# Second chunk's output projection by seven block products, with its weight factors made in steps behind keys and attention

## The chip, the cores and the metric

The kernel runs on one core of a Trainium2 chip. The metric is the device time of one execution in microseconds. The profile comes from one execution taken by the hardware profiler; times inside it are counted from the start of its span.

## The reference, cut to what matters

The layer works on x of 2048 positions by 1024 channels in float32. The part that is changed is the projection `@ w_out[l]` of the sum of two gated branches; what follows it is the norm whose result feeds the up projection.

```python
h = rmsnorm(x, attn_norm[l])
z = h @ w_in[l]                       # pool | q | k | v | gate_pool | gate_attn
gates = jax.nn.sigmoid((z[..., o4:] + b_gate[l]).astype(jnp.float32))
g_pool, g_attn = gates[..., :D_MODEL], gates[..., D_MODEL:]
a = pool_mixer(u_pool, w_pool[l], pool_scale[l])
b = swa_sink_attention(q, k, v, sinks[l])

x = x + (g_pool * a + g_attn * b) @ w_out[l]

h = rmsnorm(x, ffn_norm[l])
up = causal_depthwise_conv(h @ w_up[l], conv_w[l], conv_b[l])
gate, val = up[..., :D_FF], up[..., D_FF:]
x = x + (jax.nn.silu(gate) * val) @ w_down[l]
```

## The kernel before

Activations lie with channels on the 128 partitions and positions along the row. The 2048 positions are worked on in two chunks of 1024 (`c` = 0 and 1), each in two halves of 512 columns (`N0`, `N1`). The 1024 channels are eight tiles of 128. A product in float32 is made of three matmuls in a reduced format: each operand is split into a high part (ACT copy) and a low part (DVE subtraction), and high·high, high·low and low·high are summed (`mm3`, line 262, and `product`, line 1170).

Each chunk passes through these stages:

- `mixer`: keys and values block by block, then 32 attention items (four groups of eight blocks). Between an item's scores, probabilities and values TensorE works on *fillers*, projections of queries, pooled channels and gates. The gate projections of some channel tiles are left for `gates`.
- `gates`: for each channel tile in `UNITS[c]`, the two gate projections as seven block products (a Strassen-Winograd scheme: seven products of half-size blocks instead of eight, with sums of blocks as operands). Then `combine` makes the mixed branch of that channel tile and stores it in DRAM (`xd`).
- `out_proj`: the output projection, classic. For each half of the columns and each of the eight output tiles `m`, 24 matmuls (eight channel tiles by three) go to one PSUM bank. DVE adds the residual (line 1090), ACT scales by the norm's gain (line 1091) and squares, and the result is stored in `x2d`. Weights come through `stream`: raw slab into buffer `R`, split into `U`. The last channel tiles, 0 and 1, come straight from SBUF for the first half (`x0`, lines 1395 and 1396).
- In the second half of `out_proj`, `norms` closes the sum of squares of the first half on TensorE (`rstd`, line 629), POOL raises it to the power -1/2, `spread` (line 640) spreads it over the partitions into PSUM, and `right_first` scales and splits the operands of `up` (`normed`, line 1126; `parted`, lines 1043 and 1044).
- `up`: the up projection, convolution and gate for 22 feature tiles, by seven block products each. Its first units need the operands B11 and B21, then T1 to T4 and B22 (`right_t1` to `right_t4`), all made by DVE and ACT as the first units run. The first two units' weight factors are read from DRAM (`Kept`).
- `Down`: the down projection.

The order on each engine is laid out ahead of the run by a scheduler that goes by program order as priority and takes work that is ready; `tc.issue_after` puts instructions behind a given one on its engine. Each engine then works strictly in that order. All plain transfers are issued by SP in one queue; accumulating transfers by POOL. Buffers come from pools: `up` (tag U, 19 of 8 KB a partition), `rp` (R, 3 of 4 KB), `fp` (F, 4), `mp` (M, 5), `qp` (Q, 6). PSUM has two banks each for tags f, a and t, and one pair for s. A transfer into a buffer is issued only when the buffer is free.

## Time and profile before

| | |
|---|---|
| median of 3 runs | 2409.88 us (2409.58 to 2410.88) |
| profiled execution | 2411.6 us, span 2409.9 us |
| TensorE (PE) busy | 2375.1 us, 99%, 11120 matmuls |
| DVE busy | 1885.8 us, 78% |
| ACT busy | 1180.4 us, 49% |
| POOL busy | 177.0 us, 7% |
| DMA | 400.77 MB, mean 166 GB/s |
| second chunk's keys | about 1233 to 1324 us |
| its attention, three groups and part of the fourth | 1324 to 1557 us |
| its output projection on TensorE | 1681.86 to 1771.02 us |

A line of the profile names engine, line of the kernel, instruction and operands by the program's tags, with times in microseconds unless marked ns. Matmuls are pipelined, so their listed lengths overlap; the distance between starts is what one costs.

### The profile page before, as it was taken

What the parts mean: (1) busy time and instruction counts of PE and PEld (TensorE: products, weight loads), DVE (VectorE), ACT (ScalarE), POOL (GpSimd) and SP (SyncE); (2) the same over time, 40 slices, a digit from 0 to 9 for tenths busy, and PEclk for the clock granted to TensorE, in tenths of its full rate; (3) what the DMA queues carried; (4) which work ended last, traced back from release to release, by engine and by line L of the source; (5) the groups of instructions that cost most, each with busy time, mean ns of one, the idle gap of its engine ahead of it and who ended that gap; (6) DMA issues with size and microseconds to landing.
All of it is one profiled execution on the core that took longest, in us unless ns stands there. A gap on an engine that the chain in (4) does not pass through costs nothing.

```text
span 2409.9 us, 30324 instructions
## 1 busy us (share of the span) xinstructions
PE 2375.1 (99%) x11120; PEld 1970.3 (82%) x11120; DVE 1885.8 (78%) x2916; ACT 1180.4 (49%) x2169; POOL 177.0 (7%) x122
## 2 busy tenths in 40 slices
PE   9999999999999999999999999999999999999999
PEld 8888887877888888788888888878888888888887
DVE  8687887876977777799945867787588777779994
ACT  7455455454555555543522544554546445554431
POOL 1123111000000000000002142200000000000000
PEclk9999999999999999999999999999999999999999
DMA  9767778588222333545244576665742222228421
GB/s 342 245 202 236 228 218 274 192 288 295 103 79 79 93 117 114 178 173 183 88 155 141 171 220 195 200 201 198 230 167 93 95 80 79 79 71 288 140 70 53
DMA packets 162597, 400.77 MB, mean 166 GB/s; under 512 B 14224, under 2 KB 50576, under 8 KB 152720
## 3 DMA queue, kind: packets, MB, share of 16 engines
q1 hardware_dynamic: 157664, 390.26, 47.8%
q0 software_dynamic: 4352, 8.39, 2.2%
q8 instruction: 87, 1.43, 0.2%
q14 instruction: 62, 0.51, 0.1%
q10 hardware_dynamic: 432, 0.19, 0.0%
HBM read 264.17 MB, written 134.61 MB: 165 GB/s over the span
## 4 chain that ended last, share of the span: by engine, by line
PE 53%; DMA 2%; DVE 2%; ACT 1%; issue 0%; POOL 0%; DVEq 0%; ACTq 0%; POOLq 0%; SPq 0%
PE f L262 11%; PE f L1170 11%; PE t L1170 6%; PE f L1637 4%; PE a L1637 4%; PE s L1637 4%; PE t L1637 4%; PE a L1170 3%; PE a L934 1%; PE a L262 1%; PE s L873 1%; DMA tad<-U 1%; PE t L906 0%; DMA U<-xT 0%; DMA F<-dd 0%; DMA U<-xd 0%
## 5 line engine op out<-in xcount | busy, mean ns | idle before, releaser
L262 PE MATMUL f<-U,U 128*128 128x512 f32 (+1 forms) x2880 | 674.5, 390 | 9.4 <-ACT U L245 5.3
L262 PEld LDWEIGHTS f<-U,U 128*128 128x128 f32 x2880 | 529.1, 188 | 120.5 <-ACT U L245 6.6
L1170 PE MATMUL f<-U,U 128*128 128x512 f32 x1872 | 446.9, 390 | 4.1 <-ACT Q L1188 3.8
L1170 PEld LDWEIGHTS f<-U,U 128*128 128x128 f32 x1872 | 350.4, 188 | 80.1 <-ACT Q L1188 6.0
L1236 DVE SCALAR_TENSOR_TENSOR M<-F,vc,M 128x1024 f32<-128x1024 f32 x176 | 225.1, 1281 | 140.8 <-ACT M L1233 140.5
L1170 PE MATMUL t<-U,U 128*128 128x512 f32 x1332 | 316.7, 391 | 0.6 <-ACT Q L1188 0.6
L1170 PEld LDWEIGHTS t<-U,U 128*128 128x128 f32 x1332 | 250.9, 189 | 53.3 <-ACT Q L1188 1.2
L358 ACT CAST U<-R 128x1024 fp32r<-128x1024 f32 x147 | 153.8, 1053 | 86.5 <-DVE R L387 42.3
L1170 PE MATMUL a<-U,U 128*128 128x512 f32 x756 | 183.9, 390 | 0.0
L359 DVE TENSOR_TENSOR U<-R,U 128x1024 fp32r<-128x1024 f32 x147 | 179.2, 1220 | 3.0 <-ACT U L358 3.0
L1170 PEld LDWEIGHTS a<-U,U 128*128 128x128 f32 x756 | 141.3, 188 | 29.4 <-ACT Q L1188 0.2
L1170 PE MATMUL f<-U,M 128*128 128x512 f32 x624 | 151.3, 390 | 2.1 <-DVE F L1214 2.0
L892 ACT ACTIVATE Q<-s,st,rq 128x128 f32<-128x128 f32 x256 | 113.7, 455 | 63.6 <-DVE st L889 63.2
L1170 PEld LDWEIGHTS f<-U,M 128*128 128x128 f32 x624 | 116.8, 188 | 27.7 <-DVE F L1214 3.6
L914 POOL TENSOR_SCALAR_AFFINE_SELECT M<-M 128x1024 fp32r<-128x1024 f32 x64 | 94.7, 1479 | 381.2 <-DVE st L894 245.0
L1222 ACT COPY F<-f 128x512 f32<-128x512 f32 x52 | 30.5, 586 | 182.7 <-PE f L1170 182.7
L1595 ACT CAST U<-U 128x1024 fp32r<-128x1024 f32 x76 | 79.0, 1051 | 83.4 <-PE s L1637 21.5
L1233 ACT ACTIVATE M<-F,vc 128x1024 f32<-128x1024 f32 x88 | 109.4, 1243 | 2.0 <-DVE F L1218 0.5
L1596 DVE TENSOR_TENSOR U<-U,U 128x1024 fp32r<-128x1024 f32 x76 | 91.9, 1218 | 2.8 <-ACT U L1595 2.6
L1595 ACT CAST F<-U 128x1024 fp32r<-128x1024 f32 x44 | 46.2, 1050 | 93.0 <-PE a L1637 63.5
L941 ACT COPY U<-a 128x512 f32<-128x512 f32 x64 | 37.6, 587 | 109.4 <-PE a L934 109.1
L1188 ACT COPY Q<-f 128x512 f32<-128x512 f32 x104 | 60.8, 585 | 50.8 <-PE f L1170 50.8
(281 smaller groups left out, 3728.5 us busy)
## 6 DMA issues: line engine op xcount, KB each, us to landing
R<-w_up SPq DMA_DIRECT2D x80, 512.0 KB, 3.7
actd<-M SPq DMA_DIRECT2D x44, 512.0 KB, 2.6
U<-w_down SPq DMA_DIRECT2D x88, 256.0 KB, 4.7
U<-actd SPq DMA_DIRECT2D x88, 256.0 KB, 5.0
qd<-U SPq DMA_DIRECT2D x64, 256.0 KB, 3.7
Q<-qd SPq DMA_DIRECT2D x64, 256.0 KB, 4.9
R<-w_out SPq DMA_DIRECT2D x32, 512.0 KB, 5.1
U<-kept_S SPq DMA_DIRECT2D x12, 1024.0 KB, 6.3
```

The costliest lines, as they stand in the source:

```text
L262: nc.tensor.matmul(out, a, b, start=(i == 0), stop=(i == n - 1))
L358: A.copy(t[:, 0], raw)
L359: V.tensor_sub(t[:, 1], raw, t[:, 0].bitcast(F32))
L892: A.activation(pr[:, h, :], sc[:, h, 0:P], AF.Exp, bias=nm[:, h:h + 1], scale=it["rq"][:, h:h + 1], accum_out=rs[:, h:h + 1])
L914: G.affine_select(own.rearrange("p a h q -> p (a h) q"), pa.bitcast(F32).rearrange("p a h q -> p (a h) q"), pattern=[[0, 8], [1, P]], base ...
L1170: nc.tensor.matmul(bank, a[:, x, k, :], b[k // 2][:, y, k % 2, :], start=(first and i == 0), stop=(i == 11), skip_group_check=True)
L1188: Up.last = A.copy(t, bank).ins
L1233: A.activation(y, u[:, 2:], AF.Identity, bias=cw[:, 3, m:m + 1], scale=cw[:, 2, m:m + 1])
L1236: V.scalar_tensor_tensor(y, u[:, j:j + T], cw[:, j, m:m + 1], y, op0=ALU.mult, op1=ALU.add)
L1595: A.copy(hi, src)
L1596: V.tensor_sub(lo, src, hi.bitcast(F32))
L1637: nc.tensor.matmul(into[m], u[:, 0, c_], v[:, 1], start=(first and j == 0), stop=(k == n - 1 and j == 2), skip_group_check=True)
```

## The change

In the second chunk (`c` = 1) the output projection is no longer done by `out_proj` but by `out_blocks`. The output tiles 0 to 3 and 4 to 7 are the two row halves, the channel tiles 4 to 7 ("one") and 0 to 3 ("two") the halves of the sum, `N0` and `N1` the column halves. Seven products of blocks, each 48 matmuls to four PSUM banks, replace the 384 matmuls of the classic form. Their order is A11·B11, A12·B21, S2·T2, S3·T3, A22·T4, S1·T1, S4·B22.

The left factors are made by `out_factors`, a generator of 32 steps: one step after each of the eight key blocks and each of the 24 items of the first three attention groups. A step loads two slabs of `w_out`, or combines and splits one factor of 512 columns and stores it in DRAM (`out_parts`, 2 MB for each of the seven). `Out.weights` reads two 1 MB tiles back for each product.

The right operands come from `xd` through `mixed`, for channel tiles 0 and 1 too. Four PSUM banks `x` sum products 1, 3, 4 and 5, four banks `y` hold product 2, then 6 and 7. `kept` copies `x` to SBUF at half scale and adds the residual by an accumulating transfer issued by POOL; `final` adds a bank to that, squares it and stores it to `x2d`. The result stays in SBUF as operand of `up` without the norm's gain, so `normed` applies gain and scale by two instructions of 512 columns (`Halves`). The order of the mixing units in the second chunk becomes 5, 2, 4, 3, 0, 1. The entries of `w_out` for the second chunk leave the weight stream.

```diff
-UNITS = {0: (5, 2, 3, 0, 1), 1: (5, 2, 3, 4, 0, 1)}
+UNITS = {0: (5, 2, 3, 0, 1), 1: (5, 2, 4, 3, 0, 1)}
...
-        out += [("out", m) for n in range(2) for m in range(KT)]
+        out += [("out", m) for n in range(2) for m in range(KT) if c == 0]
...
+PRODUCTS = (("A11", "B11"), ("A12", "B21"), ("S2", "T2"), ("S3", "T3"), ("A22", "T4"),
+            ("S1", "T1"), ("S4", "B22"))
...
+    out_parts = {name: dp.tile([P, 4, 2, 4, P], F32, f"wo_{name}") for name, _ in PRODUCTS}
+    def out_factors():
+        one, two = slice(4, 8), slice(0, 4)
+        for i in range(4):
+            g, v = (rp.tile([P, 8, P], F32, "R") for _ in range(2))
+            load(g, w_out[i])
+            load(v, w_out[i + 4])
+            def part(name, src, i=i):
+                t = rp.tile([P, 2, 4, P], F32R, "R")
+                A.copy(t[:, 0], src)
+                V.tensor_sub(t[:, 1], src, t[:, 0].bitcast(F32))
+                load(out_parts[name][:, i], t.bitcast(F32))
+            yield
+            part("A11", g[:, one])
+            yield
...
+            V.tensor_sub(v[:, one], g[:, one], v[:, one])
+            V.tensor_sub(v[:, two], v[:, two], v[:, one])
+            part("S3", v[:, one])
+            yield
...
     def normed(x, n, pb):
...
+        if isinstance(x, Halves):
+            for k in range(2):
+                t, m = x.parts[n][:, k], 2 * x.j + k
+                V.scalar_tensor_tensor(t, t, vc[:, V_FN + m:V_FN + m + 1], pb[:, 0:512],
+                                       op0=ALU.mult, op1=ALU.mult)
+            return
...
+        def weights(self):
+            name = PRODUCTS[len(self.w)][0]
+            ts = [up_.tile([P, 2, 2, 4, P], F32R, "U") for _ in range(2)]
+            for i, t in enumerate(ts):
+                load(t.bitcast(F32), out_parts[name][:, 2 * i:2 * i + 2])
+            self.w.append(ts)
+        def mul(self, i, banks, first=False, by_pair=False):
+            w, r = self.w[i], self.b[PRODUCTS[i][1]]
+            for n in range(8):
+                j, m = divmod(n, 4) if by_pair else divmod(n, 2)[::-1]
+                at = 0
+                for k in range(2):
+                    for a, b in ((0, 0), (0, 1), (1, 0)):
+                        nc.tensor.matmul(banks[m], w[m // 2][:, m % 2, a, (2 * j + k + 2) % 4],
+                                         r[j][:, b, k], start=(first and j == 0 and at == 0),
+                                         stop=(j == 1 and at == 5), skip_group_check=True)
+                        at += 1
+                yield n
+        def kept(self, h, n, banks):
+            x = self.xs[h, n] = up_.tile([P, 4, 512], F32, "U")
+            for m in range(4):
+                A.activation(x[:, m], banks[m], AF.Copy, scale=0.5)
+            for i in range(2):
+                m = slice(2 * i, 2 * i + 2)
+                G.dma_start(x[:, m], self.rest(h, n)[:, m], accum_op=ALU.add)
+        def final(self, h, n, m, bank):
+            x = self.xs[h, n][:, m]
+            V.scalar_tensor_tensor(x, bank, 0.5, x, op0=ALU.mult, op1=ALU.add)
...
+            load(x2d[4 * h + m][:, n * 512:n * 512 + 512], x)
+    def out_blocks(ob):
+        heads = [Kept(f) for f in PRE]
...
+        s = ps2.tile([P, T], F32, "s")
+        x = [s[:, 0:512], s[:, 512:T]] + [ps.tile([P, 512], F32, t) for t in "at"]
+        ob.weights()
+        ob.mix()
+        run(0, x, True, True)
+        ob.first(2)
+        right_t1(ob.m, ob.b, None)
+        ob.mix()
+        ob.kept(0, 0, x)
+        ob.weights()
+        ob.first(3)
+        y = [ps.tile([P, 512], F32, t) for t in "ffta"]
+        run(1, y, True, True)
+        t2s = right_t2(ob.m, ob.b, None)
+        ob.weights()
+        for m in range(4):
+            ob.final(0, 0, m, y[m])
+        run(2, x)
+        right_t3(ob.m, ob.b)
+        ob.kept(0, 1, x)
+        ob.weights()
+        run(3, x)
+        right_t4(ob.m, ob.b, t2s)
+        ob.residual(1, 0)
+        ob.kept(1, 1, x)
+        ob.weights()
+        for n in ob.mul(4, x):
+            if n % 2 == 1:
+                ob.final(1, 0, n // 2, x[n // 2])
+        right_b22(ob.m, ob.b)
+        ob.weights()
...
+        for n in ob.mul(5, y, True):
+            if n == 2:
+                stats(0)
+            if n == 5:
+                pb = whole(0)
+            if n % 2 == 1:
+                ob.final(1, 1, n // 2, y[n // 2])
+        xg = ob.pairs()
+        for j in range(2):
+            right_first(xg, b, j, pb)
+        for n in ob.mul(6, y):
+            if n == 0:
+                for j in range(2, 4):
+                    right_first(xg, b, j, pb)
+            if n == 3:
+                for f in range(2):
+                    heads[f].fetch("A11", "A12")
+                stream.ahead().step(1)
+            if n % 2 == 1:
+                ob.final(0, 1, n // 2, y[n // 2])
+        return xg, b, [lambda: stats(1), lambda: whole(1)], heads
...
-            if f == n - 1:
+            if f == n - 1 and c > 0:
+                ob = Out(c)
+                for _ in range(2):
+                    ob.mix()
+                ob.weights()
+            elif f == n - 1:
                 mixes = {j: mixed(j) for j in (3, 2, 1)}
...
+        parts = out_factors() if c > 0 else iter(())
...
+            next(parts, None)
             if n > 1 or n == c == 1:
                 turn(n - 1)
...
+            if group < 3:
+                with tc.issue_after(last):
+                    next(parts, None)
...
-        up(c, *out_proj(c, *ms), dn)
+        up(c, *(out_blocks(*ms) if c > 0 else out_proj(c, *ms)), dn)
```

More of the change, by code (lines that the diff above doesn't have):

```diff
@@ L1135, in right_t1 @@
             normed(xg[j], 1, pb)
[L1136 removed]
+            q11, q12 = half(xg[j], 0), half(xg[j], 1)
             V.tensor_sub(q11, q12, q11)
@@ L1173, in product, with __init__, mix, first @@
                 i += 1
+    class Out:
+        def __init__(self, c):
+            self.c, self.m, self.w, self.b, self.xs = c, [], [], {}, {}
+            self.accs = [[], []]
+        def mix(self):
+            j = 3 - len(self.m)
+            self.m.append(Halves(j, [mixed_half for t in [mixed(j)]
+                                     for mixed_half in (t[:, :, N0], t[:, :, N1])]))
+        def weights(self):
[4 more added lines that the diff above has]
+            self.w.append(ts)
+        def first(self, j):
+            right_first(self.m, self.b, j, None)
+        def mul(self, i, banks, first=False, by_pair=False):
[10 more added lines that the diff above has]
+                yield n
+        def rest(self, h, n):
+            return xT[4 * h * P:(4 * h + 4) * P, self.c * T + n * 512:self.c * T + n * 512 + 512] \
+                .rearrange("(k p) t -> p k t", p=P)
+        def kept(self, h, n, banks):
[5 more added lines that the diff above has]
+                G.dma_start(x[:, m], self.rest(h, n)[:, m], accum_op=ALU.add)
+        def residual(self, h, n):
+            x = self.xs[h, n] = up_.tile([P, 4, 512], F32, "U")
+            load(x, self.rest(h, n))
+        def final(self, h, n, m, bank):
+            x = self.xs[h, n][:, m]
+            V.scalar_tensor_tensor(x, bank, 0.5, x, op0=ALU.mult, op1=ALU.add)
+            accs = self.accs[n]
+            if not accs:
+                accs.append(fp.tile([P, 512], F32, "F"))
+                A.square(accs[0], x)
+            else:
+                sq = mp.tile([P, 512], F32, "M")
+                A.square(sq, x)
+                if h == 1 - n and m == 3:
+                    accs.append(sq)
+                else:
+                    V.tensor_add(accs[0], accs[0], sq)
+            load(x2d[4 * h + m][:, n * 512:n * 512 + 512], x)
+        def pairs(self):
+            return [Halves(j, [self.xs[j // 2, n][:, j % 2 * 2:j % 2 * 2 + 2] for n in range(2)])
+                    for j in range(4)]
@@ new lines, in out_blocks, with run, stats, whole @@
+    def out_blocks(ob):
+        heads = [Kept(f) for f in PRE]
+        def run(*a, **kw):
+            for _ in ob.mul(*a, **kw):
+                pass
+        s = ps2.tile([P, T], F32, "s")
[29 more added lines that the diff above has]
+        ob.weights()
+        stream.fetch(stream.used + 1)
+        stream.part(stream.used + 1)
+        norms, b = [], {}
+        def stats(n):
+            rstd(ob.accs[n], r2[:, 4 * n:4 * n + 4])
+        def whole(n):
+            return spread(r2[:, 4 * n:4 * n + 4], None)
+        for n in ob.mul(5, y, True):
[19 more added lines that the diff above has]
+        return xg, b, [lambda: stats(1), lambda: whole(1)], heads
@@ L1490, in gates @@
             old.combine()
-            if f == n - 1:
+            if f == n - 1 and c > 0:
+                for j in range(2):
+                    ob.first(j)
+            elif f == n - 1:
                 ms = {j: [parted(mixes[j][:, :, N0])] for j in (3, 2, 1)}
```

34 lines of the change are left out of this document (26 added, 8 removed).

## The prediction

> **What bounds the kernel now.** I read the page first, then the tensor engine alone in order of time around the second chunk's output projection, then stages, then the last unit before it and the first units after it.
>
> ```profile
> span 2409.9 us, 30324 instructions
> PE 2375.1 (99%) x11120; PEld 1970.3 (82%) x11120; DVE 1885.8 (78%) x2916; ACT 1180.4 (49%) x2169; POOL 177.0 (7%) x122
> ```
> The tensor engine is busy for 2375.1 of 2409.9 us. Only 34.8 us are idle in the whole run, so a gain must come from fewer matmuls, and anything that makes it wait shows one for one.
>
> ```profile
> 1657.06 2.88 PE L1170 MATMUL t<-U,U 128*128 128x512 f32 x12
> 1659.78 2.88 PE L1170 MATMUL f<-U,U 128*128 128x512 f32 x12
> ...
> 1681.86 5.38 PE L262 MATMUL f<-U,U 128*128 128x512 f32 x23
> 1687.57 49.53 PE L262 MATMUL f<-U,U 128*128 128x512 f32 x217 [0.33 <-ACT U L1395]
> 1736.93 0.95 PE L629 MATMUL a<-one,F 128*128 128x1 f32 x8
> 1737.74 13.23 PE L262 MATMUL f<-U,U 128*128 128x512 f32 x57
> 1750.81 0.60 PE L640 MATMUL s<-identr,M 128*128 128x128 f32 x4
> 1751.16 20.02 PE L262 MATMUL f<-U,U 128*128 128x512 f32 x87
> 1771.02 2.88 PE L1170 MATMUL f<-U,U 128*128 128x512 f32 x12
> 1773.74 0.28 PE L629 MATMUL a<-one,F 128*128 128x1 f32 x2
> ```
> Columns: start, us, engine, line, instruction, count, idle before it with what ended it. A group of twelve starts 2.72 us after the one ahead of it, so one matmul of 512 columns takes 2.72/12 = 0.2267 us (the mean of 390 ns that the page shows is the pipelined length). The second chunk's projection is 23 + 217 + 57 + 87 = 384 matmuls of line 262 from 1681.86 to 1771.02, 89.2 us; 384 x 0.2267 is 87.0. The other 2.1 us are, by the starts, two blocks of small matmuls (0.81 and 0.35 us) and about 0.6 us at the front, where the first channel tile waits for the last mixing unit's parts.
>
> ```profile
> 1324.00:1557.00 233.00, 231.44 (x1203) 195.90 (x1204) 177.93 (x355) 110.29 (x354) 62.11 (x38) 1.00 0.64 193
> 1657.00:1682.00 25.00, 24.97 (x110) 20.35 (x110) 18.41 (x21) 11.34 (x16) 0.00 (x0) 1.00 0.73 258
> 1682.00:1771.00 89.00, 88.67 (x397) 73.08 (x396) 56.27 (x79) 44.56 (x73) 1.04 (x1) 1.00 0.67 220
> ```
> The columns after the window's length are busy times: PE, weight loads, DVE, ACT, POOL; then the clock, the DMA share and GB/s. The clock is full in all three. In the projection DVE has 56.3 of 89 us and ACT 44.6; DMA is the fullest helper (0.67, and 0.73 just before).
>
> **The removed matmuls.** The new stage runs 7 products of 8 groups of 6 matmuls: 336 instead of 384. That is 48 x 0.2267 = **-10.9 us**. [...]
>
> **The front.** The first product is A11·B11. It needs channel tiles 4 to 7 only, whose units end well before 1681.9 in the new order 5, 2, 4, 3, 0, 1. The 0.6 us wait goes: **-0.6**. Late next are channel tiles 0 and 1, which now reach TensorE through DRAM: the second half of product 2 needs `first(3)`, and that needs the load of `mixed(0)` behind the last `combine`.
>
> ```profile
> 1685.28 1.94 SPq L239 DMA_DIRECT2D xd<-M  x2
> 1686.11 0.75 DVE L1387 SCALAR_TENSOR_TENSOR M<-M,vc,M 128x512 f32<-128x512 f32 x1
> ...
> DMA to landing us min/median/max: 2.0/4.0/9.9
> U<-xd SPq DMA_DIRECT2D x8, 1024.0 KB, 7.1
> L1043 ACT CAST U<-U 128x1024 fp32r<-128x1024 f32 x50 | 52.2, 1052 | 40.1 <-DVE U L1126 9.8 <-DVE U L1137 8.2 <-PE t L1170 7.1
> L1044 DVE TENSOR_TENSOR U<-U,U 128x1024 fp32r<-128x1024 f32 x50 | 60.6, 1219 | 7.5 <-ACT U L1043 7.2
> ```
> The last half is combined at 1686.9. Its store takes from 2.0 us, so it lands at about 1689.1, and the 1 MB load behind it takes 5 (an estimate for a quiet queue, the median is 7.1): 1694.1 to 1696.2. The copy to the high part takes 1.05 and the subtraction 1.22, which gives 1696.4 to 1698.5. TensorE reaches that half after 72 matmuls, at 1681.9 + 16.3 = 1698.2. So it is met or missed by little. The load and the weight loads of the next products share one queue, so I take **+1.2** with bounds of 0 and 4 (a load of 10 us). One product later `right_t2` has 2 to 3 us to spare, and the remaining operands (T3, T4, B22) are made a product or more ahead.
>
> **PSUM and the accumulated residuals.** `kept` reads four banks by ACT copies, and `final` reads four by DVE. Each bank is rewritten 8.2 us (six groups of 1.36) or more after its last matmul, and a copy takes 0.62 (line 245's row below). I count nothing for it; without that cover each would cost its own 0.6 us four times a product. The accumulating transfers run on POOL's queue, where nothing else stands but the small powers of the norm.
>
> ```profile
> q1 hardware_dynamic: 7010, 19.28, 71.0%
> GB/s 197 234 291 269 276 223 200 422 354 245 219 144 232 230 246 149 45 110 274 280 318 341 203 324 354 223 70 185 18 159 101 0 155 219 194 356 335 437 401 411
> q0 software_dynamic: 4352, 8.39, 2.2%
> tad<-U POOLq DMA_DIRECT2D x16, 512.0 KB, 7.8
> ```
> The first two rows are of the 82 us from 1690 to 1772, the others of the whole run. The stage moved 19.28 MB at a share of 0.71, so 331 GB/s while busy, with slices up to 437. Accumulating transfers are dearer: 8.39 MB took 2.2% of 2410 us on all engines, 158 GB/s, and half a megabyte 7.8 us to land. The new stage moves 12.6 MB of factors for products 2 to 7 (two of 1 MB each), 4.2 of x2d stores, 2.1 of heads, 2.1 of mixes, 1.0 of residual and 1.6 of up weights, 23.6 MB in all: 71 us at 331 GB/s. Another 3.15 MB are accumulated: 20 us. That is 91 us against a stage of 78. What saves it is the lead. Of the 19 buffers of `up`, the mixing units give back 14 operand tiles and their weights between 1657 and 1682, so by my count of buffers factors 1 to 3 are asked for before 1682 and each later pair two products (21.8 us) ahead of use, where a 1 MB load took 7.1. The accumulated blocks are wanted one to four products later. I count no stall beyond the 1.2 above, and keep this as a rival.
>
> **Norm and the start of up.** `stats(0)` now sums two accumulators instead of one: 0.81 us more on TensorE, **+0.8**. The parts of B for `up` were made over four channel tiles of the old second half. Now all four `right_first` calls stand behind `whole(0)`, six groups into product 6.
>
> ```profile
> L1090 DVE SCALAR_TENSOR_TENSOR M<-f,F 128x512 f32<-128x512 f32 x32 | 22.0, 687 | 33.7 <-PE f L262 27.9 <-issue 5.6
> L375 DVE TENSOR_TENSOR M<-R,M 128x512 fp32r<-128x512 f32 x49 | 33.9, 691 | 0.2 <-ACT M L374 0.2
> ...
> 1776.90 0.43 DVE L638 COPY M<-r 128x512 f32<-128x512 f32 x1 [1.13 <-POOL r L622]
> 1778.25 0.60 PE L640 MATMUL s<-identr,M 128*128 128x128 f32 x4
> 1778.89 2.35 DVE L1126 TENSOR_TENSOR U<-U,s 128x1024 f32<-128x1024 f32 x2 [1.56 <-PE s L640]
> 1795.43 1.21 DVE L1044 TENSOR_TENSOR U<-M,U 128x1024 fp32r<-128x1024 f32 x1
> 1796.70 1.01 PEld L1170 LDWEIGHTS f<-U,U 128*128 128x128 f32 x5 [0.31 <-DVE U L1044]
> ```
> From the stage's start the product ends lie 10.9 us apart. `stats(0)` runs at 54.4 + 4.1 = 58.5, and the scale is spread by about 65. From there DVE owes: two `final` of product 6 (0.69 + 0.69 each, 2.8), four `right_first` (two scalings of 512 columns, 0.75 by the timeline's row at 1686.11, and 1.22: 2.7 each, 10.8), four `final` with three sums of product 7 (4.8), and one weight part (1.2): 19.6 us. The stage ends at 336 x 0.2267 + 1.6 + 0.35 = 78.1, so the last square is there at 65 + 18.4 = 83.4, some 5.3 us into `up`; before, the sums ran 2.7 us in (1773.74). `u1.one` fills that gap. But behind it DVE goes without a pause from the scaling at 1778.89 to T2's last part at 1796.64, and TensorE already waits for that part at 1796.70 (0.31). The chain starts 2.6 later, less the 0.9 that the transposes had waited for TensorE (1777.33 to 1778.25), plus four scalings that are two of 0.75 instead of one of 1.2 (0.27 each, 1.1): 2.8, and a wait already stands at its end. **+2.8**; 0 if DVE's order puts the `final` steps ahead of the last two `right_first`, 5 if the weight parts queue in front too.
>
> **The factors in steps.** 28 parts (ACT copy 0.62, DVE subtraction 0.69 by line 375's row), 16 combinations (0.69), 8 loads of 0.5 MB and 28 such stores (18.9 MB, 57 us of DMA at 331 GB/s). That adds 30 us to DVE and 17 to ACT over 32 steps, eight behind keys and 24 behind attention.
>
> ```profile
> L245 ACT CAST U<-R 128x512 fp32r<-128x512 f32 x122 | 69.6, 620 | 9.5 <-DMA R<-w_out 4.3 <-DMA R<-w_poolT 2.9 <-issue 1.4
> ...
> 1322.00:1330.50 8.50, 7.68 (x39) 6.13 (x38) 8.30 (x18) 5.19 (x20) 1.03 (x1) 1.00 0.11 32
> 1424.00:1432.50 8.50, 8.50 (x45) 7.19 (x44) 8.27 (x17) 3.95 (x14) 3.11 (x2) 1.00 0.84 229
> 1543.00:1551.50 8.50, 7.82 (x41) 6.41 (x40) 8.36 (x16) 5.13 (x13) 2.04 (x1) 1.00 0.18 70
> ```
> In attention DVE is at 177.9 of 233 us; 24 steps add 23, which makes 86%. The DMA share goes from 0.64 to about 0.83. SP's queue gets 36 more issues; a store waiting for its part holds the query loads behind it, but these are asked for two items (17 us) ahead. `R` has three buffers and two hold the slabs, so each part waits for the store ahead of it to land, 4.0 us by the median of the `xd` row, out of some 8.5 us for one item. In the fullest stretches of that length DVE has 8.3 of 8.5 us already, and there a step pushes the chain from scores to values back by up to 1.3 us. Most of that is covered by projections on TensorE. **+1.0**, bounds 0 and 6 (a quarter of a microsecond lost at each of the 24 steps).
>
> **Sum.** -10.9 - 0.6 + 1.2 + 0.8 + 2.8 + 1.0 = -5.7 us. The profiled span is 2409.9 (its execution 2411.6 with what lies around it); the median of the runs is 2409.88, the same as the span. So 2409.9 - 5.7 = **2404.2 us**. All costs at their low ends give -10.7 (2399.2), all at the high ends -10.7 + 4 + 5 + 6 = +4.3 (2414.2).
>
> **Rivals.** *Full gain, 2399.2*: DVE's order and the load of channel tiles 0 and 1 both fit. For it: DVE and ACT are idle for 33 and 44 of the 89 us that the projection takes now, so they have room. Against it: the wait at 1796.70 already stands at the end of the DVE chain.
>
> *Attention crowded, 2409.2*: the full items spill onto TensorE what exceeds 8.5 us, 1.1 each in the three shown and the like in others, 6 us in all instead of 1.0. For it: two of the three stretches shown have TensorE at 7.7 and 7.8 of 8.5. Against it: over 1324 to 1557 TensorE lost 1.6 us in all, and the one at 1424 with 8.27 us of DVE lost none.
>
> *Transfers bound the stage, slower, 2417*: the place is products 2 to 5, the price 91 us of transfers against 78 of matmuls, +13 on the forecast; it decides once buffers come back so late that the factors lose their two-product lead. For it: the share before the stage is already 0.73. Against it: 2 MB of weights and one mix leave that stretch, factor tiles are 8 KB to a row, and slices of such loads show over 400 GB/s. [...]
>
> *The change doesn't do what it says*: if the projection's matmuls do not drop by 48, only the costs of 5.8 us less the front's 0.6 remain, 2415.1. The loops count 7 x 48, so hardly any chance.
>
> **Chances.** Forecast 0.46, full gain 0.21, attention crowded 0.19, transfers bound 0.12, no drop 0.02. A measurement of this kernel can tell about 0.2% from no change, 4.8 us, so faster means below 2405.1 and slower above 2414.7. The forecast's own range is 2401.5 to 2407; about three quarters of it are below 2405.1. Faster: 0.21 + 0.35 = 0.56. Slower: 0.12 + 0.02 = 0.14. The rest, 0.30, is no change. The range for 8 in 10 runs from 2398.8 to 2411.5: it takes in the full gain and the crowded attention and leaves out most of the transfer-bound case.
>
> **What would show it.** Matmuls of line 262 fall by 384, and 336 appear under the new `mul`. Right: they span about 79 us, the gap before product 2's second half is under 1.5 us, and the wait for DVE at T2 in `up` grows from 0.3 to about 3. Wrong: idle TensorE inside products 3 to 7 that ends on a DMA of `wo_` (transfers), more than 3 us of new waits on POOL or DVE between 1233 and 1557 (attention), or no longer wait at T2 (full gain).

## The result and the profile after

The changed kernel takes 2424.2 us (median of 4 runs, 2422.9 to 2425.6), the kernel before beside it 2410.4 (2409.6 to 2411.1). The ratio is 1.0056, with a 95% interval of 1.0044 to 1.0069: slower, by 13.8 us, and outside the range that was forecast (2398.8 to 2411.5).

The page after (its head and one group), and two stretches of the trace, attention and the block stage, which is the new output projection (columns as before: length, busy times of PE, weight loads, DVE, ACT, POOL; clock, DMA share, GB/s):

```profile
span 2421.1 us, 30322 instructions
PE 2370.1 (98%) x11080; PEld 1962.8 (81%) x11080; DVE 1907.9 (79%) x2948; ACT 1181.4 (49%) x2166; POOL 186.5 (8%) x128
...
L266 PE MATMUL f<-U,U 128*128 128x512 f32 (+1 forms) x2496 | 586.6, 390 | 9.6 <-ACT U L249 4.8
```
```profile
1314.00:1567.00 253.00, 242.67 (x1257) 202.85 (x1256) 205.31 (x403) 123.04 (x380) 64.40 (x39) 1.00 0.76 238
...
1689.00:1776.00 87.00, 82.38 (x360) 67.36 (x359) 48.23 (x59) 32.18 (x46) 8.40 (x7) 0.96 0.77 247
```
The matmuls went as counted: line 262's 2880 of the old page are 2496 of line 266, and TensorE is busy 5.0 us less. But the span is 11.2 us longer. TensorE is idle some 10 us in attention, and 4.6 us in the block stage, where the mean clock is 0.96 (1.00 in the projection before).

Where it was lost can be read from the starts of the stages on TensorE (first transpose of attention, first unit product behind it, first matmul of the output projection, first product of `up`), here for the first profiles (the kernels are told below). "Clock" is 1 minus the granted clock, summed over stretches of 1 us from 1300 us on to 10 us before the end; half clock while TensorE waits counts too, so it is the most that the clock can have cost.

| kernel | attention | gates | output proj. | rest | clock | span | median against before |
|---|---|---|---|---|---|---|---|
| before | 242.2 | 123.8 | 89.2 | 638.9 | 0 | 2409.9 | 2410.4 |
| after | 253.1 | 122.2 | 86.6 | 645.2 | 5.1 | 2421.1 | +13.8 |
| a_plain | 252.5 | 122.3 | 79.5 | 643.7 | 3.4 | 2412.7 | +5.2 |
| b_steps | 253.4 | 122.4 | 89.0 | 638.9 | 0 | 2420.1 | +9.4 |
| c_blocks | 242.8 | 123.0 | 85.6 | 646.5 | 5.1 | 2413.1 | +4.6 |
| d_both | 242.7 | 122.2 | 79.5 | 642.4 | 0 | 2402.4 | -3.6 |
| e_moves | 242.9 | 122.8 | 88.9 | 639.0 | 0 | 2409.6 | +0.2 |
| f_math | 249.6 | 122.8 | 89.0 | 639.2 | 1.7 | 2417.2 | +5.7 |

So the changed kernel loses 10.8 us in attention, wins 2.6 in the projection where 10 were expected, and loses 6.3 behind it. It wins 1.6 in the gates. The other 1.8 lie ahead of the change: in the first chunk the clock column, counted the same way, is 5.1 in the profile of before and 3.4 in that of after, and waits differ by some tenths.

Inside the block stage, rows picked from the timelines of PE, DVE, ACT and POOL, in order of time:

```profile
1689.30 2.88 PE L1260 MATMUL s<-U,U 128*128 128x512 f32 x12
...
1699.16 1.23 POOL L1277 DMA_DIRECT2D U<-xT  x1 [101.63 <-PE a L1260]
1712.12 0.69 DVE L1285 SCALAR_TENSOR_TENSOR U<-f,U 128x512 f32<-128x512 f32 x1 [4.93 <-DMA U<-xT]
1712.35 1.22 POOL L1277 DMA_DIRECT2D U<-xT  x1 [11.95 <-issue]
1719.22 2.88 PE L1260 MATMUL t<-U,U 128*128 128x512 f32 x12
1721.10 0.69 DVE L1285 SCALAR_TENSOR_TENSOR U<-t,U 128x512 f32<-128x512 f32 x1 [6.56 <-DMA U<-xT]
1721.71 1.22 DVE L1084 TENSOR_TENSOR U<-U,U 128x1024 fp32r<-128x1024 f32 x1
1721.83 0.63 ACT L1292 ACTIVATE M<-U 128x512 f32<-128x512 f32 x1 [6.62 <-DVE U L1285]
1724.70 1.07 ACT L1274 ACTIVATE U<-s 128x512 f32<-128x512 f32 x2
1725.82 8.63 PE L1260 MATMUL s<-U,U 128*128 128x512 f32 x24 [3.71 <-ACT U L1274]
1726.18 1.22 POOL L1277 DMA_DIRECT2D U<-xT  x1 [12.62 <-ACT U L1274]
1734.28 2.88 PE L1260 MATMUL a<-U,U 128*128 128x512 f32 x12
1737.26 1.22 POOL L1277 DMA_DIRECT2D U<-xT  x1 [9.86 <-issue]
1749.12 1.21 POOL L1277 DMA_DIRECT2D U<-xT  x1 [10.64 <-PE a L1260]
1757.11 1.22 POOL L1277 DMA_DIRECT2D U<-xT  x1 [6.78 <-issue]
```
Read it from the PE row at 1725.82 back. Product 4 waits 3.71 us for ACT's copies of product 3's banks (`kept`). ACT does them at 1724.70, because it works in order and ahead of them stand squares of `final`'s sums (line 1292). Those wait for DVE's `final`, and DVE waits in order for the accumulated residual, 4.93 and 6.56 us; T3's split (1721.71) stands behind it too. POOL's two transfers of one pair are 13 us apart with nothing between them. Over the whole stage the waits of DVE are:

```profile
DVE U L1285 <- DMA U<-xT: 20.2, 4, 6.6
```
(20.2 us in four waits.) The second thing in the PE row is its length: 24 matmuls take 8.46 us to the next start, where 24 x 0.2267 are 5.44. The granted clock there:

```profile
1720.00:1724.00 4.00, 2.10 (x10) 1.41 (x8) 2.90 (x4) 1.56 (x2) 0.00 (x0) 1.00 0.19 70
1724.00:1728.00 4.00, 2.18 (x5) 1.80 (x6) 3.24 (x5) 3.84 (x6) 1.22 (x1) 0.64 0.81 207
1728.00:1732.00 4.00, 4.00 (x11) 3.03 (x11) 1.58 (x2) 0.64 (x2) 0.00 (x0) 0.50 0.96 347
```
From 1725.1 to 1732 the clock is half. The first 0.7 us of that still lie in the wait; after it the matmuls lose 8.46 - 5.44 = 3.0 us. The wait of 3.71 us therefore cost 6.7.

Behind the stage:

```profile
1775.87 2.99 PE L1225 MATMUL f<-U,U 128*128 128x512 f32 x12 [0.91 <-issue]
1780.65 0.35 PE L669 MATMUL a<-one,F 128*128 128x1 f32 x2 [1.79 <-DVE F L1296]
...
1807.79 1.43 PE L1225 MATMUL f<-U,U 128*128 128x512 f32 x5 [1.82 <-DVE U L1084]
```
The sum of squares is late by 1.79 us, and behind it the clock is half for 3.4 us (1783 to 1787, 1.7 in the clock column); T2 is late by 1.82, where before it was 0.31.

In attention, what PE waited for, and then two of ACT's waits:

```profile
PE t L946 <- DVE Q L938: 4.4, 6, 1.9
PE s L913 <- ACT Q L932: 4.3, 4, 1.7
```
```profile
ACT R L406 <- DMA wo_A<-R: 7.0, 4, 3.1
...
ACT R L406 <- DMA wo_S<-R: 3.0, 3, 1.7
```
Before, the like rows of PE were 1.1 and 0.4 us in all. A factor step's copy waits on ACT until the store of the part before it has let the R buffer go, and ACT's exponentials stand behind it.

### The profile page after: what moved, and what is told of

Same layout as the page of the kernel before. It is cut to its first block, busy times and chain, and to the rows that moved or that the text cites. A ratio compares the mean times of both kernels' runs of the same rounds, so it can differ in the third digit from the quotient of the medians.

```text
span 2421.1 us, 30322 instructions
## 1 busy us (share of the span) xinstructions
PE 2370.1 (98%) x11080; PEld 1962.8 (81%) x11080; DVE 1907.9 (79%) x2948; ACT 1181.4 (49%) x2166; POOL 186.5 (8%) x128
## 4 chain that ended last, share of the span: by engine, by line
PE 47%; DVE 4%; DMA 3%; issue 3%; ACT 1%; POOL 0%; SPq 0%; POOLq 0%; DVEq 0%; ACTq 0%
PE f L1225 11%; PE t L1225 6%; PE f L266 5%; PE f L1846 4%; PE a L1846 4%; PE s L1846 4%; PE t L1846 4%; PE a L1225 3%; PE a L266 1%; DMA U<-xT 1%; DVE F L1030 1%; PE a L974 1%; PE s L1260 1%; DMA tad<-U 1%; PE s L913 1%
## 5 line engine op out<-in xcount | busy, mean ns | idle before, releaser
L266 PE MATMUL f<-U,U 128*128 128x512 f32 (+1 forms) x2496 | 586.6, 390 | 9.6 <-ACT U L249 4.8
L266 PEld LDWEIGHTS f<-U,U 128*128 128x128 f32 x2496 | 457.2, 188 | 105.2 <-DVE U L250 7.3
L1225 PEld LDWEIGHTS f<-U,U 128*128 128x128 f32 x1872 | 351.1, 188 | 83.5 <-ACT Q L1387 5.5
```

The lines of the kernel that those rows point to most:

```text
L266: nc.tensor.matmul(out, a, b, start=(i == 0), stop=(i == n - 1))
L1225: nc.tensor.matmul(bank, a[:, x, k, :], b[k // 2][:, y, k % 2, :], start=(first and i == 0), stop=(i == 11), skip_group_check=True)
```

## The experiments

**Two losses, taken away alone and together.** First the way of the residual:

```diff
         def kept(self, h, n, banks):
...
             x = self.xs[h, n] = up_.tile([P, 4, 512], F32, "U")
+            load(x, self.rest(h, n))
             for m in range(4):
-                A.activation(x[:, m], banks[m], AF.Copy, scale=0.5)
-            for i in range(2):
-                ... G.dma_start(..., accum_op=ALU.add)
+                V.scalar_tensor_tensor(x[:, m], banks[m], 0.5, x[:, m], op0=ALU.mult, op1=ALU.add)
```


> The changed kernel with one thing undone in the output stage: the residual of the three kept blocks comes by a plain load on SP's queue, and DVE adds half the product's bank to it, instead of four copies by ACT and two accumulating transfers by POOL. The factor steps in keys and attention stay. Theory A (the accumulating transfers run one after the other, each 9 to 13 us, and what waits for them on DVE, 20.2 us in four waits, holds ACT and the banks of products 4 to 7 and the start of the next stage): the waits of DVE on the accumulated blocks go, the output stage falls from 86.6 us to 79 to 81, the start of the next stage gives back 2 to 5 us more, total 2410 to 2416. Rival B (the stage is held by the bytes of 21 MB of factors and by DVE's own work, so the way the residual comes does not matter, and DVE even gets 12 instructions more): the stage stays at 85 to 89 us, total 2421 to 2427.

Measured: +5.2 us against before (ratio 1.0021, 1.0012 to 1.0030), so 8.6 better than the change. The stage takes 79.5 us, no product waits longer than this:

```profile
1707.81 2.56 PE L1260 MATMUL f<-U,U 128*128 128x512 f32 x10 [0.61 <-DVE U L1084]
```
Theory A holds, and with more bytes on the same queue and 12 instructions more on DVE. DVE still waits 9.7 us in three waits for the plain loads (20.2 in four before), but no product waits for what stands behind them. The gain behind the stage is smaller than it said (1.5 us, not 2 to 5).

Then the factor steps alone, with the old projection and the old order of units behind them:

```diff
-UNITS = {0: (5, 2, 3, 0, 1), 1: (5, 2, 4, 3, 0, 1)}
+UNITS = {0: (5, 2, 3, 0, 1), 1: (5, 2, 3, 4, 0, 1)}
...
-        up(c, *(out_blocks(*ms) if c > 0 else out_proj(c, *ms)), dn)
+        up(c, *out_proj(c, *ms), dn)
```


> The factor steps are made in keys and attention and stored as in the changed kernel, but the second chunk's output projection is the old one, with the old order of gates; the stored factors are not used. Theory (the steps cost what the trace of attention shows, +10.8 us, whatever the stage behind does with them): before plus 9 to 13 us, 2419 to 2424, of which attention shows 9 to 11. Rival (the growth of attention comes mostly of the new order of gates and of the later loads that the block stage brings with it): before plus 0 to 4 us, 2410 to 2415.

Measured: +9.4 us (1.0033, 1.0021 to 1.0046), attention 253.4 us, everything behind it as before:

```profile
1316.00:1558.00 242.00, 232.95 (x1208) 194.89 (x1206) 196.63 (x386) 118.61 (x369) 62.44 (x37) 1.00 0.75 239
```
and of before:

```profile
1316.00:1558.00 242.00, 240.44 (x1257) 203.47 (x1256) 186.54 (x369) 111.86 (x360) 62.28 (x39) 1.00 0.62 188
```
PE is busy for 233.0 us of the same 242, where it was 240.4, and DVE for 10 us more. The steps cost what attention shows; the order of gates and the later loads do not.

The block stage without the steps, and with both edits. Both runs load stored factors of the gates in place of those of `w_out`, so their output is not the reference's, and only their time counts:

```diff
-                load(t.bitcast(F32), out_parts[name][:, 2 * i:2 * i + 2])
+                load(..., kept[i]["A11", "A12"]...)
...
-        parts = out_factors() if c > 0 else iter(())
+        parts = iter(())
```


> The block products of the changed kernel without the making of their factors: no steps in keys and attention, and each product loads, in the same transfers, factors of the gates that are in DRAM already, so the output differs from the reference's. What is left is the change's own stage at its full price. Theory (10.8 us of the loss come of the steps): the changed kernel minus 9 to 12, 2411 to 2415, about the time of before, for the stage gains 2.6 us and the start of the next loses 6.2. Rival (the stage and its transfers cost more than the steps): 2417 to 2422.

> Both edits at once: no factor steps (factors of the gates are loaded in their place, so the output differs from the reference's), and the residual by plain loads with the sum on DVE. Theory (two losses that add: steps 10.8 us, accumulating transfers 8 to 13 us): 2398 to 2404, which is the full gain of 10.2 us that I had computed for 48 matmuls fewer and the x0 wait. Rival (the two share a cause, for example a DVE that is full in both places, so that taking both away gives no more than the larger one): 2408 to 2414.

Measured: +4.6 us (1.0017, 1.0008 to 1.0027) and -3.6 us (0.9979, 0.9970 to 0.9988). Taking away the steps wins 9.2, the accumulating transfers 8.6, both 17.4: the losses are separate and add. With both gone the stage takes 79.5 us, and the profiled run is 7.5 us under the profile of before; the median says only 3.6, 2.9 over the range that was expected: its ten runs lie between 2401.6 and 2408.8, with granted clocks from 0.999 down to 0.996. Behind the stage of the run with both edits one wait is new:

```profile
1788.95 1.43 PE L1225 MATMUL f<-U,U 128*128 128x512 f32 x5 [1.83 <-DVE U L1084]
```
It is the wait for T2 again.

**Work or transfers in the steps.** One run in which a step only moves data, and one in which it stores nothing:

```diff
-                t = rp.tile([P, 2, 4, P], F32R, "R")
-                A.copy(t[:, 0], src)
-                V.tensor_sub(t[:, 1], src, t[:, 0].bitcast(F32))
-                load(out_parts[name][:, i], t.bitcast(F32))
+                for h in range(2):
+                    load(out_parts[name][:, i, h], src)
```


> As the run with the old projection and the factor steps (attention 253.4 us against 242.2 before, total 9.4 us over before), but a step only moves data: it reads its slabs of w_out and stores the half slab twice to the factor's place, with no copy by ACT and no subtraction by DVE, so no factors are made (they are not used in this run either). Theory M (the steps cost by their transfers: 4 x 1 MB in, 28 x 0.5 MB out, buffers R held longer, later loads of queries, gates and inputs): attention 250 to 254 us, total 7 to 10 us over before. Rival W (they cost by the 28 copies on ACT and the 40 subtractions on DVE, put in order ahead of the chain of scores, probabilities and values): attention 242 to 245 us, total 0 to 3 over before.

```diff
-                load(out_parts[name][:, i], t.bitcast(F32))
```


> The other half of the same pair: the steps read their slabs and do all their work on ACT and DVE, but store nothing (so no factors are kept; they are not used here). Theory M: attention 242 to 246 us, total 0 to 4 us over before. Rival W: attention 250 to 254 us, total 7 to 10 over before. If both runs lie in the middle (246 to 249), the two add, and neither alone is the cause.

Measured: +0.2 us (0.9999, 0.9990 to 1.0009) and +5.7 (1.0027, 1.0016 to 1.0038), attention 242.9 and 249.6 us. The first does not test what it was meant to. With no engine's work to wait for, the scheduler put the transfers ahead, at 1120 to 1233 us, behind the down projection:

```profile
1120.00:1160.00 40.00, 40.00 (x176) 32.81 (x175) 39.50 (x59) 14.37 (x18) 0.00 (x0) 1.00 0.96 328
```
(before: a share of 0.33). It shows that 18.9 MB cost nothing there, not what they cost in attention. The second run does tell, and lies between its two theories: ACT's and DVE's work alone makes 7.4 us of attention. The stores, in the run with both, add 3.8 more (253.4 against 249.6), which fits the waits for R. The split is rough: 1.7 of the 7.4 are clock behind a wait of 1.95 us, and the attention of the run with both has no such piece. The medians give 5.7 for the work and 3.7 for the stores.

**Why the accumulating transfers run one by one.** Twice the scratch memory that the program asks for (`dynamic_dma_scratch_size`, 2048 for 1024), with one Q buffer of six given up for it:

```diff
-    qp = pool("qp", 6)
+    qp = pool("qp", 5)
...
-    nc = bacc.Bacc(..., dynamic_dma_scratch_size=1024)
+    nc = bacc.Bacc(..., dynamic_dma_scratch_size=2048)
```


> [...] In the changed kernel POOL issued its six accumulating transfers 13.2, 13.8, 11.1, 11.9 and 8.0 us after one another. If the small memory makes one wait for the one before it, the two of a pair come less than 3 us apart, DVE's waits on accumulated blocks shrink from 20.2 us to under 10 and the output stage from 86.6 to 80 to 83 us; in attention the lost Q buffer may cost some us. If each transfer waits for the one before for another reason, the spacing stays at 8 to 13 us and the stage at 86 to 88.

Measured: 2418.6 us (one run), and on POOL:

```profile
1700.25 1.23 POOL L1277 DMA_DIRECT2D U<-xT  x1 [102.06 <-PE a L1260]
1702.48 1.20 POOL L1277 DMA_DIRECT2D U<-xT  x1 [1.00 <-DVE U L1218]
1723.41 1.21 POOL L1277 DMA_DIRECT2D U<-xT  x1 [19.73 <-PE t L1260]
1726.28 1.22 POOL L1277 DMA_DIRECT2D U<-xT  x1 [1.66 <-ACT U L1274]
```
The first two pairs go out 2.2 and 2.9 us apart instead of 13.2 and 11.1, DVE waits 12.0 us for them, not 20.2 (under 10 was expected), and the stage falls to 81.4 us. It was that memory which made one transfer wait for the one before. The lost Q buffer does not show in attention (253.0).

**Other places for the factors.** The residuals are plain in all that follow. First, 16 steps behind the last group of the first chunk's down projection, with their subtractions on POOL, and 16 in keys; then with the copies on POOL too:

```diff
+                if self.c == 0 and g == len(self.groups) - 1:
...
+                    side[0] = G
+                    if at % 2 == 0 and at // 2 < 16:
+                        next(factor_steps, None)
...
-                V.tensor_sub(t[:, 1], src, t[:, 0].bitcast(F32))
+                side[0].tensor_sub(t[:, 1], src, t[:, 0].bitcast(F32))
```


> A version that should beat both: the residual by plain loads with the sum on DVE, and the factor steps moved out of attention. 16 of the 32 steps lie behind every second product of the last group of the first chunk's down projection (1120 to 1230 us, where POOL is idle and the transfers of the run that only moves data cost nothing), with their subtractions on POOL and the copies on ACT; the other 16 lie in keys, two behind each block of rows, on ACT and DVE. The output is the reference's. Theory (steps cost only where DVE, ACT and the chain of attention have no slack): attention falls from 252.5 to 242 to 244 us, the down projection and keys keep their times within 2 us, total 2403 to 2409, 2 to 7 us under before. Rival (POOL's subtractions slow DVE, which is 98% busy in the down projection, or ACT's copies wait for R buffers in order ahead of the next parts): the down projection grows by 4 to 10 us and eats the gain, total 2408 to 2416.

> As that run, but in the down projection POOL also makes the copies, so that ACT has no part in the 16 early steps and cannot wait for a buffer in order. Theory: 2403 to 2409, equal to it within 1 us, if ACT's waits there cost nothing. Rival: 2 us or more under it if ACT's waits held the down projection; 2 us or more over it if POOL, with twice the work, becomes late and the steps run into keys.

Measured: +14.0 us (1.0059, 1.0045 to 1.0073) and +18.0 (1.0077, 1.0064 to 1.0089). The rival, in both halves. Attention does fall to 243.2 us in both, but the first transpose of keys comes 17.4 and 21.9 us later than before. The same subtraction of the down projection, on DVE from 1120 to 1200 us, before and, in the first of the two, with POOL working beside it, and POOL's own (1120 to 1240 us):

```profile
L1596 DVE TENSOR_TENSOR U<-U,U 128x1024 fp32r<-128x1024 f32 x18 | 21.7, 1216 | 0.1
```
```profile
L1807 DVE TENSOR_TENSOR U<-U,U 128x1024 fp32r<-128x1024 f32 x15 | 22.5, 1517 | 0.9 <-ACT U L1806 0.9
...
L409 POOL TENSOR_TENSOR R<-R,R 128x512 fp32r<-128x512 f32 x14 | 24.7, 1768 | 190.5 <-ACT R L408 190.5
```
DVE's instruction takes 1517 ns for 1216, and DVE was 97% busy there before. It is not the transfers: in the run that only moves data the DMA share is 0.94 over these 80 us, and the instruction takes 1220 ns:

```profile
L1789 DVE TENSOR_TENSOR U<-U,U 128x1024 fp32r<-128x1024 f32 x18 | 21.7, 1220 | 1.2 <-ACT U L1788 1.2
```
ACT waited up to 16.2 us for a store to free R. PE lost 9.2 us in one wait on DVE at the start of keys.

Next, the plain blocks A11, A12, A22 stored by the first chunk's projection, which splits those slabs anyway, and S1 to S4 made in keys, two in a block; then with the parts in M buffers:

```diff
+                if c == 0 and n == 1:
+                    for name, k in (("A11", 4), ("A12", 0)) if m < 4 else (("A22", 0),):
+                        load(out_parts[name][:, m % 4], w[:, :, k:k + 4].bitcast(F32))
```


> A second try at a version that beats both, with no work on POOL and none in attention. The residual comes by plain loads. The 12 factors that are plain blocks of w_out (A11, A12, A22) are not made by steps at all: the first chunk's output projection splits the same slabs anyway, and in its second half stores the parts (6.3 MB) as it has made them. The other 16 (S1 to S4, 16 copies on ACT, 32 subtractions or additions on DVE, 8.4 MB out) are made in keys, two in each block of rows, half a block apart. Theory (keys has room: PE is 100% busy there with DVE at 59% and ACT at 32%, and the 8 steps that the changed kernel has there cost it nothing): keys stays at 82.5 us within 2, attention at 242 to 244, total 2404 to 2409, 2 to 6 us under before. Rival (16 steps wait for slabs and for the one R buffer left for parts, in order ahead of the keys' own chain, as the early steps of the two runs before did): keys grows by 4 to 12 us, total 2411 to 2420.

> As that run, with one thing else: the parts that a step makes lie in an M buffer (five of them) instead of the third R buffer, so that a step need not wait for the store of the one before it. Theory: equal to it within 1 us, if no step waits there. Rival: 2 us or more under it, if the waits for the store cost it; over it, if the M buffers are missed by the queries that are made in keys.

Measured: +5.3 us (1.0029, 1.0016 to 1.0041) and +8.9 (1.0038, 1.0025 to 1.0051). In the profile of the first, keys (82.5 us) and attention (242.5) are as before: 16 parts cost nothing in keys. This profile is of the fastest of its six runs (2411.8 us), with a span equal to that of before; what makes the median longer is not in it. The gain of the block stage is lost in the first chunk, whose stores filled the queue, and in the start of `up`; keys began 4.7 us later than before:

```profile
598.85 1.65 PE L1221 MATMUL f<-U,U 128*128 128x512 f32 x3 [2.49 <-DMA U<-kept_A]
```
In the second, keys takes 84.4 and attention 248.8 us, with 4.2 us of waits of PE on loads of made weights between the two.

Then the plain blocks split in the block stage, out of raw slabs; in a second run two of the three splits stand earlier:

```diff
+                if name[0] == "A":
+                    r = rp.tile([P, 2, 4, P], F32, "R")
+                    ... load(r[:, j], w_out[at + 2 * i + j][:, k:k + 4])
...
+                A.copy(t[:, :, 0], r)
+                V.tensor_sub(t[:, :, 1], r, t[:, :, 0].bitcast(F32))
```


> A third try at a version that beats both. The run before this one had keys at 82.5, attention at 242.5 and the block stage at 79.6 us in its profile, and lost 4.6 us in the first chunk's output projection, to the stores of A11, A12 and A22 (transfers 79% busy there against 57%, and a 2.5 us wait of PE on a late load behind them). Here these three factors are never stored: the block stage loads the slabs of w_out themselves (half the bytes) into R buffers, which it does not use otherwise, and splits them there, six copies of 1024 elements on ACT and six subtractions on DVE of 1.2 us. S1 to S4 are made in keys, two in a block. Theory: first chunk as before, keys and attention as before within 1 us, the block stage 79.5 to 82 us for DVE is 73% busy in it, the start of the next stage 3 to 5 us over before; total 2403 to 2408, 2 to 7 us under before. Rival (the 7 us more on DVE meet its full stretch at the end of gates and at the start of the block stage, and PE waits over 3 us on a split part): 2410 to 2416.

> The run that splits A11, A12 and A22 in the block stage, with the splits of two of them earlier: A12's slabs are loaded and split behind the last gate products (before the stage, where DVE was 62 to 85% busy), A22's are loaded one product earlier and split ahead of the T4 operands instead of behind them. Theory (PE's waits of 4.4 and 2.5 us and the two and one slow-clock windows behind them came of the place of these two splits): no wait of PE over 1 us in the stage, stage 79.5 to 82 us, total 2404 to 2410. Rival (DVE has no room for 7 us more there, wherever they stand): the waits move to product 1 or 3 or to the end of gates, total 2412 to 2419.

Measured: +8.1 us (1.0035, 1.0023 to 1.0047) and +4.1 (1.0015, 1.0006 to 1.0024). Keys and attention are as before in both. In the first, PE waits for `first(3)` in product 2, and again ahead of product 5, for `kept`'s sums of product 4, with 5.1 us of clock at the two. What ended last ahead of the second wait was no split but a load of the residual, for which DVE waited 3.43 us:

```profile
1704.69 4.63 PE L1269 MATMUL f<-U,U 128*128 128x512 f32 x10 [4.38 <-DVE U L1077]
...
1735.16 1.29 DVE L1284 SCALAR_TENSOR_TENSOR U<-s,U 128x512 f32<-128x512 f32 x2 [3.43 <-DMA U<-xT]
1736.59 4.58 PE L1269 MATMUL s<-U,U 128*128 128x512 f32 x12 [2.50 <-DVE U L1284]
```
The second run loses the later wait and keeps the first one, of 4.39 us: its raw slabs go into SP's queue ahead of the mixed channel tiles and wait there for R, and DVE waited 2.9 us for the load of these tiles (1688.70), from which on it worked without a pause up to the operand that PE missed. The stage took 92.4 us in the first and 86.4 in the second.

Last, all 28 parts in keys, 24 (A22 split in the block stage), and 20 (A11 and A12 stored by the first chunk):

```diff
             block_b(n)
+            next(parts, None)
...
                 turn(n - 1)
+            next(parts, None)
+            if n % 2 == 1:
+                next(parts, None)
```


> The run with plain residuals, with one thing else: all 28 factor steps in keys, three or four in each of its 8 blocks, none in attention. Theory (only the place counts: PE leads in keys, with DVE at 59% and ACT at 32% before, and 28 steps add 28 us of DVE and 18 us of ACT to 82 us): keys 82.5 to 84, attention 242 to 244, total 2404 to 2409. Rival (keys has its own bound: 14.7 MB out and 4.2 MB in beside its 12 MB is 380 GB/s, the steps wait for the one R buffer of parts, some 4 us each by the stores' time to landing, and push the last steps and the queries into attention): keys plus attention grow by 4 to 10 us, total 2411 to 2417.

> As that run with 24 steps in keys, three in a block: the four for A22 are left out, and the block stage loads the plain slabs for its fifth product and splits them there on ACT and DVE (1720 to 1730 us, where DVE is about half busy). Theory: keys 82.5 to 83.5, attention 242 to 243.5, the stage 79.5 to 81, total 2403 to 2408. Rival as in the run before, with 24 parts for 28: 2409 to 2415; or the split of A22 holds product 5 as the splits of the run with plain slabs held products 2 and 4 (4.4 and 2.5 us): 2409 to 2413 with keys and attention as in the theory.

> The run that stores the plain parts in the first chunk's output projection and makes S1 to S4 in keys, with one difference: the four parts of A22 are made in keys too (20 there, two or three a block), so that the first chunk stores 4.2 MB for 6.3. Theory: the wait on the late load in the first chunk falls from 2.5 us to under 1, keys and attention stay as they were with 16, total 2405 to 2411. Rival (20 parts in keys are over its bound): the loads of made weights and queries behind them come late, PE waits 2 us or more at the start of attention, total 2413 to 2420.

Measured: +14.1 us (1.0056, 1.0044 to 1.0069), +12.4 (1.0050, 1.0036 to 1.0063) and +14.1 (1.0054, 1.0042 to 1.0067). Keys itself stays at 82.5 us in all three. But the loads for the start of attention, which share SP's queue with the stores, come late. SP issues in order, and a store waits for DVE to finish its part. First the wait of PE with 24 parts, then the waits of SP's queue for parts, in us in all, times and the longest, from the start of keys to 1335 us, with 24 and with 16 parts:

```profile
1328.72 2.47 PE L266 MATMUL f<-U,U 128*128 128x512 f32 x5 [8.27 <-DMA U<-made_q]
```
```profile
SPq L243 <- DVE R L407: 42.0, 14, 6.7
```
```profile
SPq L243 <- DVE R L407: 19.3, 4, 8.0
```
Attention takes 261.2, 258.7 and 256.6 us, with 5.1, 6.8 and 3.4 us of clock in it. The rival holds: keys has its own bound. 16 parts fit with R buffers (with M buffers attention grew), 20 do not. No kernel that really makes its factors beat the kernel before.

## Why the prediction was wrong, by its own steps

**The removed matmuls, the front, `first(3)`: right.** The terms -10.9, -0.6, +1.2 and +0.8 give -9.5 for the projection. With plain residuals and no steps it went from 89.2 to 79.5 us, -9.7. The gap before product 2's second half was nil after the change, and 0.6 with plain residuals (priced at 1.2, forecast under 1.5). That the sum agrees to 0.2 us is in part luck, for this term was half of what was priced and some tenths elsewhere make up for it. (Of the 2.1 us beyond the matmuls that the prediction reads in the old projection, the three items it names make 1.8.)

**The start of `up`: the size right without the accumulating transfers, the place in part.** +2.8 forecast; +3.5 measured with both losses gone (638.9 to 642.4). The wait at T2 that was named grew from 0.31 to 1.83 us, not to about 3; another 0.87 us is a wait ahead of the spreading of the scale (line 680), and about 1 us is not located.

**PSUM and the accumulated residuals: the first step that failed.** The text said "I count nothing" and that the blocks "are wanted one to four products later". It had the right row (7.8 us for half a megabyte, 20 us in all) and then asked only whether POOL's queue was free. It did not ask who stands behind `final` on DVE. The transfers went out 8.0 to 13.8 us apart, so the last of six was issued at 1757. DVE stood still for 20.2 us, and behind it stood T3's split, the squares on ACT and, behind those, the copies that let the next product have its banks. That is 7.1 us in the stage and 1.5 at the start of `up` by the pair of runs, 8.6 in all where 0 was written.

**The clock: not in the prediction at all.** Of the 7.1 us 3.7 are the wait, 3.0 are TensorE at half clock behind it, and 0.9 are a gap ahead of `up`; the run with plain residuals has 0.6 of its own at product 2. Every wait was priced at its own length.

**The factors in steps: the second step that failed, by size and by bound.** +1.0 with bounds of 0 and 6 was written; attention grew by 10.8 and the runs with and without steps differ by 9.2 to 9.4. The mechanism was named: full stretches of DVE and the single R buffer for parts. It was priced as if the projections on TensorE covered it. The bound of a quarter of a microsecond a step came from no row; the row-based figure in the same paragraph, up to 1.3 us where a stretch is full, would have allowed far more. Measured in the profiles of attention, 7.4 us come with the work alone (1.7 of it clock), which PE shows as waits for DVE and ACT inside the chain of scores, probabilities and values, and 3.8 are added by stores. The rival *attention crowded* had the right place with 6 us.

**Transfers bound the stage: not shown.** It had the right sign for another reason. No product waited on a load of factors in the changed kernel or with plain residuals, though the latter's queue carried more. What had to do with transfers were six small ones on POOL.

**The sum.** From profile to profile: -9.7 + 7.1 in the projection, +6.3 behind it (3.5 of its own, the rest about the late sum of squares with its clock), +10.8 in attention, -1.6 in the gates, which the prediction did not touch, and -1.8 ahead of it all: +11.2. Most of the -1.6 is one wait of TensorE for DVE, before and after:

```profile
1602.36 3.01 PE L1170 MATMUL f<-U,M 128*128 128x512 f32 x12 [1.68 <-DVE F L1214]
```
```profile
1610.16 3.04 PE L1225 MATMUL f<-U,M 128*128 128x512 f32 x12 [0.50 <-DVE F L1413]
```
The second chunk's order of units cannot explain it alone, for with the old order the gates show -1.4 too and this wait is 0.4; why it shrinks stays open.

## What to carry to other kernels

Ask of each wait that a change adds what stands behind it in order on the waiting engine, and who waits for that; a transfer that is wanted "a product later" holds everything queued behind its reader. Where TensorE is 99% busy, price its waits above their length: in the six profiles named in the next section every wait of 2.78 us or more from 50 us on went with half clock for at least 3.4 us, and some shorter ones did, down to 0.86 us. Work moved out of a stage needs a place with room on all of its engines, its buffers and its queue at once, and only a run shows how much fits there (here 16 parts in keys, not 20).

## What the runs showed of the hardware that was not expected

**The clock falls in steps of 1.7 us.** In six profiles (before, after, the run that splits two of the plain blocks earlier, and those with 28, 24 and 20 parts in keys), away from the last 10 us, the clock goes to half for 3.4 us or a multiple of it: 1 minus the clock, summed over 1 us stretches, comes in pieces of 1.71, of 3.41 and, with the wait of 8.27 us in the run with 24 parts, of 6.83. Each stands in or behind waits of TensorE; in the changed kernel 3.41 with the wait of 3.71 us and 1.71 with the one of 1.79. Length alone does not decide. From 50 us on every wait of 2.78 us or more has a piece. Shorter ones have it or not: the same wait of 0.90 us near 561 us has one in the run with 24 parts and none in the profile of before, where a wait of 2.05 us (421 us) has none either. In the changed kernel the clock falls at 1725.1, 3.0 us into the wait of 3.71 us, but in the run with 24 parts a wait of only 0.86 us (it ends at 1782.29) has a piece. Because the first chunk has such waits too, two profiles of the same code there can differ by 1.7 us: a wait near 400 us has 3.41 before (2.79 us long) and 1.71 after (2.80).

**Accumulating transfers wait for one another** with `dynamic_dma_scratch_size` at 1024: pairs 13.2 and 11.1 us apart, 2.2 and 2.9 with 2048 (the third pair 8.0 and 5.0).

**POOL's subtractions slow DVE.** 1768 ns for 512 columns on POOL, where DVE takes 691, and DVE's own of 1024 columns went from 1216 to 1517 ns beside it. Those of its additions that read one operand from PSUM were not slowed: 512 columns took 680 ns before (line 1651) and 679 beside POOL (line 1867), where 512 columns with both operands in SBUF (lines 1593 and 1804) went from 682 to 1021.
